# Half of retention's gates computed by block products, with retention's chunk in another order

## The chip, the cores and the metric

The kernel runs on one core of one Trainium2 chip. A core has TensorE (PE, matrix products into PSUM, which has eight banks), VectorE (DVE), ScalarE (ACT), GpSimd (POOL) and SyncE (SP, whose queue issues most DMAs). Each engine works through its own instructions in program order; semaphores let one wait for another. The metric is the time of one execution in microseconds (us) on the device.

## The reference

A decoder block on 1024 tokens of width 1024. After a modulated RMS norm, one wide projection `w_in` gives queries, keys, values and gates for four retention heads (key width 256, value width 512), queries, keys and values for twelve attention heads, and two merging gates. What the change touches, cut to its core:

```python
proj = h @ w_in
rq, rk, rv, rg = parts[0], parts[1], parts[2], parts[3]      # rg: 2048 gate columns, 512 a head
def step(state, inp):                                        # chunks of 128 tokens, 8 a head
    qi, ki, vi = inp
    s = einsum(qi, ki) * inner_decay
    o = einsum(s, vi) + einsum(qi, state) * q_decay
    state = state * chunk_decay + einsum(ki * k_decay, vi)
    return state, o
ro = (ro - mean(ro)) * rsqrt(var(ro) + GN_EPS)               # per head and token
ret_out = (silu(rg) * (ro * gn_g + gn_b)) @ w_ret_out
```

Then come dilated attention in three groups, the gated merge, an output projection, and an MLP with squared ReLU, each with its norm. The conditioning vector gives 48 column sets of modulation factors, `silu(c) @ w_ada`.

## The kernel before

**Arithmetic.** Each float32 operand is split into a rounded high half (ACT) and the remainder as low half (DVE); a product is three PE matmuls, low x high, high x low and high x high (`mm3`, L197). The rows L201, L203 and L205 of the profile are these three. A block of 128 input columns by 512 tokens takes three matmuls of 512 columns.

**Block products.** The class `Blocks` (L220 on) computes a pair of column sets (256 outputs) over 1024 inputs and 1024 tokens as a two by two block product with seven products in place of eight: sums of blocks of the weights (DVE), split halves, seven times four `mm3`, and sums of the results. A pair takes 7 x 4 x 3 = 84 matmuls; the plain way takes 2 x 48 = 96. `queries_keys` (L1072) runs 18 such pairs, in the order of `PAIRS` (L999): "r" rotated retention queries and keys, "a" attention queries, "g" merging gates (sigmoid). Results go to DRAM. `values` (L1182) follows: 14 products by blocks of retention's values, each of four parts `p`, whose results `v_post` (L1152) writes to DRAM; the low halves of the next weights come between the parts.

**Retention.** `chunk` (L672) is called for four heads h and eight chunks c; g = 8h + c. Everything is scheduled by hand: each engine executes in the order of the program's text. A chunk has, on PE: `kv` (keys by values, six matmuls), gate products `rg` (a set of 128 gate columns, 48 matmuls, over two chunks, 24 each), scores and key transposes of the next chunk (`s_kt`, L616), output `o` (six matmuls with the state, three with the scores), and transposes of the normalized result of the chunk before (`on_T`, L649). On DVE: the state update (two halves), the score steps, the keys' low half, the state's low half, mean and variance of `o`, the normalization itself (L728) at the chunk's end, and a modulation product (`mod_prep`, L449), one in each of 32 chunks. On ACT: high halves, copies of the transposed result, SiLU of a finished gate set (L732), and `u_final` (L660), which scales a set of the head before. On POOL: the low half of the next query and key tile `j` (L613) and a power. `ahead(2)` (from `Steps.run`, L72) splits the weights and does the modulation product of the next step at the place where it is called: in the middle of the chunk, ahead of `s_kt`. `fetch` (L583) loads queries, keys and values three chunks ahead.

**PSUM.** In retention four of the eight banks form two double tiles ("mm", `ps_mm`, L160), which the gate sets use in turn; the other four are single tiles ("s", `ps_s`, L163), taken in the order in which they come free by `kv` (two), `sT`, `kT`, `o` and `oT`. Before retention all eight banks are single tiles.

**The way in.** `values` ends with closing the memory pool of its tiles, opening retention's pool over the same memory (`open_ret`, L514), fetching chunks 1 and 2, scores of chunk 0 (`s_kt(0)`) and the new PSUM pool (`banks(False)`). A tile of the new pool waits until the old tiles under it are done with.

Of the kernel before, what the change touches and what calls it, by code (L numbers as in the profile page):

```python
# [40 lines left out]
CS_QD = 132  # L41
CS_QD2 = 136
# [92 lines left out]
def block_kernel(ctx, tc, io, stop=None, dbg=None):  # L135
# [342 lines left out]
    def proj_mm(ps, w, ks=range(NK)):  # L478
        outs = ps if isinstance(ps, list) else [ps[:, 0, :], ps[:, 1, :]]
        for k in ks:  # L480
            mm3(outs, wk(w, k), hx[k], k == 0, k == NK - 1)
# [32 lines left out]
    def open_ret():  # L514
        x_ctx.close()
        R["p"] = ret_ctx.enter_context(tc.tile_pool(name="ret", bufs=1, reuse_waits="tile"))
        R["state"] = R["p"].tile([P, 2, DV], F32, name="state")
        R["sh"] = R["p"].tile([P, 2, DV], F32R, name="stateh")
        R["sl"] = R["p"].tile([P, 2, DV], F32R, name="statel")

    def etile(name, dt=F32):
        return R["p"].tile([P, 1024], dt, tag="E", bufs=12, name=name)
# [82 lines left out]
    def jit_qk(i):  # L605
        src = hd["qk", i]
        if i > 1:
            t = R["p"].tile([P, 2, 4, C], F32R, tag="j", bufs=2, name=f"j{i}")
# [7 lines left out]
    def s_kt(i):  # L616
# [15 lines left out]
        sm = p.tile([P, C], F32, tag="sm", bufs=1, name=f"sm{h}{c}")  # L632
        smh = p.tile([P, C], F32R, tag="smh", bufs=2, name=f"smh{h}{c}")
        sml = p.tile([P, C], F32R, tag="sml", bufs=2, name=f"sml{h}{c}")
        nc.scalar.copy(sm, ps[:, :C])  # L635
        nc.vector.tensor_add(sm, sm, ps[:, C:2 * C])
        nc.vector.tensor_mul(sm, sm, decay[:, h * C:(h + 1) * C])
        nc.scalar.copy(smh, sm)
        nc.vector.tensor_sub(sml, sm, fv(smh))
        hd["s", g] = (smh, sml)  # L640
        if pk is not None:
            kd = ct[:, CS_KDEC + h:CS_KDEC + h + 1]
            kh = p.tile([P, 2, P], F32R, tag="kh", bufs=1, name=f"kh{h}{c}")
            kl = p.tile([P, 2, P], F32R, tag="kl", bufs=1, name=f"kl{h}{c}")
            nc.scalar.mul(kh, pk, kd)
            nc.vector.scalar_tensor_tensor(flat(kl), flat(pk), kd, fv(flat(kh)), op0=ALU.mult, op1=ALU.subtract)
            hd["k", g] = (kh, kl)
# [12 lines left out]
    def u_final(h, es=range(4)):  # L660
        for e in es:
            i = h * 4 + e
            t = hd["on", h][e]
            for hf in range(2):
                neg = 16 if hf == i % 2 else 0
                b = t[:, 512 * hf:512 * hf + 512]
                nc.scalar.activation(b, b, AF.Identity, scale=gnv[0][:, neg + i:neg + i + 1],
                                     bias=gnv[1][:, neg + i:neg + i + 1])
            nc.vector.tensor_mul(t, t, hd["srg", h, e])
            nc.sync.dma_start(y_d[:, 2 * (i % 2):2 * (i % 2) + 2, i // 2], t.rearrange("p (t x) -> p t x", t=2))  # L670

    def chunk(h, c, ahead, w=None):  # L672
# [4 lines left out]
        if c % 2 == 0:  # L677
            hd["rgw"] = w
            hd["rgp"] = ps_mm(f"rg{h}{c}")
        ks = range(4 * (c % 2), 4 * (c % 2) + 4)  # L680
        if g == 0:
            proj_mm(hd["rgp"], hd["rgw"], ks)
        vh, vl = hd["v", g][:, 0], hd["v", g][:, 1]
        st, sh, sl = R["state"], R["sh"], R["sl"]
        kvs = []
        if c < NC - 1:
            kh, kl = hd["k", g]
            for i in range(2):
                kv = ps_s(f"kv{h}{c}{i}")
                mm3([kv], (kh[:, i, :], kl[:, i, :]), [(vh, vl)], True, True)  # L690
                kvs.append(kv)
        if g > 0:
            proj_mm(hd["rgp"], hd["rgw"], ks[:2])
        for i, kv in enumerate(kvs):
            if c == 0:
                nc.vector.tensor_copy(st[:, i, :], kv)
            else:
                nc.vector.scalar_tensor_tensor(st[:, i, :], st[:, i, :], float(GAMMA[h] ** C), kv,
                                               op0=ALU.mult, op1=ALU.add)
        ahead(2)  # L700
# [8 lines left out]
        if c < NC - 1:  # L709
            for i in range(2):  # L710
                nc.scalar.copy(sh[:, i, :], st[:, i, :])
                nc.vector.tensor_sub(sl[:, i, :], st[:, i, :], fv(sh[:, i, :]))
        if g + 2 < NG:
            jit_qk(g + 2)
        if g > 0:
            on_T(*divmod(g - 1, NC))
        if g > 0:
            proj_mm(hd["rgp"], hd["rgw"], ks[2:])
# [5 lines left out]
        nc.vector.tensor_scalar(gr, ba[:, 1:2], ct[:, CS_QD2 + h:CS_QD2 + h + 1], GN_EPS, op0=ALU.mult, op1=ALU.add)  # L724
        nc.gpsimd.tensor_tensor(gr, gr, mhalf[:, 0:1], op=ALU.pow)
        nc.vector.tensor_mul(gr, gr, ct[:, CS_QD + h:CS_QD + h + 1])
        on = p.tile([P, DV], F32, tag="on", bufs=1, name=f"onm{h}{c}")
        nc.vector.tensor_scalar(on, po, ba[:, 0:1], gr, op0=ALU.subtract, op1=ALU.mult)  # L728
        hd["o", h, c] = on
        if c % 2 == 1:  # L730
            hd["srg", h, c // 2] = etile(f"srg{h}{c // 2}")
            nc.scalar.activation(hd["srg", h, c // 2], flat(hd["rgp"]), AF.Silu)  # L732
        if h > 0 and c < 4:
            u_final(h - 1, (c,))
# [264 lines left out]
    PAIRS = [{"r": r_pairs, "a": a_pairs, "g": g_pairs}[i].pop(0) for i in "rargrargrargrargaa"]  # L999
# [1570 lines left out]
```

## Time and profile before

| what | us |
|---|---|
| median of three runs (2231.76 to 2233.54) | 2232.41 |
| the profiled execution | 2231.9 |
| its span, first to last instruction | 2230.1 |
| PE busy | 2168.7 |
| DVE busy | 1470.1 |
| ACT busy | 912.4 |
| POOL busy | 155.1 |
| block products of queries, keys and gates | 149 to 492 |
| values | 492 to 647.4 |
| retention | 647.4 to 970.5 |

How to read it: the profiled execution lies 0.5 us below the median. A row of the order of time has start, duration, engine, line, operation, output and inputs; in brackets, how long the engine stood idle before and what released it. A row of a group has least, median and most duration in nanoseconds. A row of stages has the stretch, its length, busy time with instructions of PE, PE's weight loads, DVE, ACT and POOL, the granted PE clock as a share of full speed, the share of the DMA engines that was busy, and GB/s. PE's matmuls overlap, so the duration of one is longer than its share of time.

### The profile page before, as it was taken

The numbers are of one execution on the slowest core, as the hardware profiler recorded it, in microseconds if no ns is written. First come the engines' busy times: TensorE is split into PE (matmuls) and PEld (weight loads), VectorE is DVE, ScalarE is ACT, GpSimd is POOL, SyncE is SP. The second block draws the span as 40 slices with busy tenths as digits, with TensorE's granted clock in tenths as the row PEclk, the third lists the DMA queues.
The fourth block names the chain that finished last, engine by engine and source line by source line (L and its number), as shares of the span: only waits on it lengthen the run. The fifth ranks groups of instructions, "written<-read, shape, count | busy, mean of one in ns | idle before, by whom it ended". The sixth has DMA issues, their size and how long they took to land.

```text
span 2230.1 us, 27097 instructions
## 1 busy us (share of the span) xinstructions
PE 2168.7 (97%) x10082; PEld 1796.1 (81%) x10082; DVE 1470.1 (66%) x2303; ACT 912.4 (41%) x1671; POOL 155.1 (7%) x176
## 2 busy tenths in 40 slices
PE   7999999999989999999999999999999999999998
PEld 5888888878868888888788788888778888788887
DVE  6756777754448778865555654676866665787845
ACT  4532233223324444544634633524444445533412
POOL 0100111000012112200000000002000000000003
PEclk9999999999999999999999999999999999999999
DMA  9869999634675556559723265654234444745322
GB/s 383 220 208 299 294 296 277 189 131 174 224 255 170 181 178 203 185 175 238 224 73 96 92 219 187 237 180 159 69 135 147 155 156 165 261 141 170 123 85 76
DMA packets 157602, 414.15 MB, mean 186 GB/s; under 512 B 27222, under 2 KB 55133, under 8 KB 153054
## 3 DMA queue, kind: packets, MB, share of 16 engines
q1 hardware_dynamic: 149598, 364.19, 46.5%
q0 software_dynamic: 7872, 48.24, 9.5%
q8 instruction: 79, 1.29, 0.2%
q14 instruction: 53, 0.43, 0.1%
HBM read 321.51 MB, written 156.13 MB: 214 GB/s over the span
## 4 chain that ended last, share of the span: by engine, by line
PE 86%; DVE 6%; DMA 4%; ACT 3%; issue 1%; POOL 0%; SPq 0%; POOLq 0%; DVEq 0%; ACTq 0%
PE qap L203 5%; PE qap L201 5%; PE qap L205 5%; PE fp L201 4%; PE fp L203 4%; PE fp L205 4%; PE rg L201 3%; PE rg L203 3%; PE rg L205 3%; PE f2a L203 2%; PE f2a L205 2%; PE f2a L201 2%; PE ak L201 2%; PE ak L203 2%; PE ak L205 2%; PE va L203 1%
## 5 line engine op out<-in xcount | busy, mean ns | idle before, releaser
L201 PE MATMUL qap<-hh,qaw 128*128 128x512 f32 x216 | 84.1, 390 | 0.4 <-DVE qat L285 0.4
L205 PE MATMUL qap<-hh,qaw 128*128 128x512 f32 x216 | 84.0, 389 | 0.0
L203 PE MATMUL qap<-hl,qaw 128*128 128x512 f32 x216 | 84.0, 389 | 0.0
L613 POOL TENSOR_TENSOR j<-qk,j 128x512 fp32r<-128x512 f32 x32 | 43.3, 1353 | 462.2 <-ACT j L612 462.2
L2029 ACT ACTIVATE a<-a 128x512 f32<-128x512 f32 x48 | 30.3, 632 | 79.5 <-DVE a L2028 79.5
L1926 POOL TENSOR_TENSOR accnf<-accnf,sqnf 128x256 f32<-128x256 f32 (+1 forms) x18 | 16.6, 921 | 620.2 <-ACT sqnf L1925 620.2
L1383 ACT ACTIVATE P<-P,ng 128x128 f32<-128x128 f32 (+1 forms) x96 | 41.9, 438 | 39.0 <-DVE ng L1380 39.0
L258 DVE TENSOR_TENSOR fw<-w1r,fw 128x512 fp32r<-128x512 f32 x48 | 32.9, 687 | 36.2 <-ACT fw L248 36.2
L2215 ACT CAST w2h<-w2s 128x512 fp32r<-128x512 f32 x36 | 22.3, 621 | 77.6 <-DVE w2s L2253 73.6
L635 ACT COPY sm<-sT 128x128 f32<-128x128 f32 x32 | 8.5, 265 | 111.0 <-PE sT L626 103.8
L201 PE MATMUL fp<-h2h,fw 128*128 128x512 f32 x128 | 50.0, 390 | 0.0
L203 PE MATMUL fp<-h2l,fw 128*128 128x512 f32 x128 | 49.8, 389 | 0.0
L205 PE MATMUL fp<-h2h,fw 128*128 128x512 f32 x128 | 49.8, 389 | 0.0
L201 PE MATMUL roa<-rh,rwl 128*128 128x512 f32 x128 | 49.8, 389 | 0.0
L203 PE MATMUL roa<-rl,rwh 128*128 128x512 f32 x128 | 49.8, 389 | 0.0
L205 PE MATMUL roa<-rh,rwh 128*128 128x512 f32 x128 | 49.8, 389 | 0.0
L1764 DVE TENSOR_TENSOR rwl<-rwl,rwh 128x1024 fp32r<-128x1024 f32 x25 | 30.2, 1220 | 29.1 <-ACT rwh L1794 29.1
L1926 POOL TENSOR_TENSOR accn<-accn,sqn 128x512 f32<-128x512 f32 x12 | 15.5, 1293 | 478.2 <-ACT sqn L1925 478.2
L201 PEld LDWEIGHTS qap<-hh,qaw 128*128 128x128 f32 x216 | 40.5, 188 | 9.2 <-DVE qat L285 0.8
L203 PEld LDWEIGHTS qap<-hl,qaw 128*128 128x128 f32 x216 | 40.5, 188 | 8.4
L205 PEld LDWEIGHTS qap<-hh,qaw 128*128 128x128 f32 x216 | 40.5, 188 | 8.4
L258 DVE TENSOR_TENSOR qaw<-wa,qaw 128x512 fp32r<-128x512 f32 x54 | 37.0, 686 | 10.0 <-ACT qaw L248 10.0
(3063 smaller groups left out, 7188.1 us busy)
## 6 DMA issues: line engine op xcount, KB each, us to landing
v<-vd SPq DMA_DIRECT2D x32, 512.0 KB, 4.8
raw<-in_w_ada_dram SPq DMA_DIRECT2D x32, 512.0 KB, 5.1
w1r<-in_w_ff_dram SPq DMA_DIRECT2D x32, 512.0 KB, 4.8
vd<-vo SPq DMA_DIRECT2D x24, 512.0 KB, 4.4
yt<-y POOLq DMA_DIRECT2D x6, 2048.0 KB, 16.5
xsd<-as SPq DMA_DIRECT2D x24, 512.0 KB, 2.7
w2r<-in_w_ff2s_dram SPq DMA_DIRECT2D x24, 512.0 KB, 7.3
em<-in_w_ada_dram SPq DMA_DIRECT2D x16, 512.0 KB, 10.2
```

What stands on the lines that cost most here:

```text
L201: nc.tensor.matmul(o, wl, xh, start=first, stop=False, skip_group_check=skip)
L203: nc.tensor.matmul(o, wh, xl, start=False, stop=False, skip_group_check=skip)
L205: nc.tensor.matmul(o, wh, xh, start=False, stop=last, skip_group_check=skip)
L258: nc.vector.tensor_sub(t[:, 512:], src, fv(t[:, :512]))
L613: nc.gpsimd.tensor_sub(t[:, 1], src, fv(t[:, 0]))
L635: nc.scalar.copy(sm, ps[:, :C])
L1383: nc.scalar.activation(v, v, AF.Exp, bias=ng[:, blk:blk + 1], accum_out=st[:, g, blk, 2 + a:3 + a])
L1764: nc.vector.tensor_sub(lo, fv(lo), fv(hi))
L1926: (nc.vector if f == 7 else nc.gpsimd).tensor_add(G["acc", key], G["acc", key], sq)
L2029: nc.scalar.activation(o, o, AF.Relu)
L2215: nc.scalar.copy(hi, src)
```

## The change

- Of each head's four gate sets the last two (256 columns) become a pair "s" in `PAIRS`: 22 pairs in place of 18, results through SiLU to DRAM (`srg_d`). Retention computes only the first two, each over four chunks (12 matmuls a chunk; in chunks 0 to 3 of head 0: 24, 12, 6 and 6), and loads the other two in chunks 6 and 7 of their head.
- Within a chunk: normalization is put off to the next chunk (`normed`, with the mean folded into a bias `nb`, and done by ACT); the transposes are of the result two chunks back; state update and state halves are done 1024 wide, both products `kv` in one double tile; the keys' halves come ahead of the scores'; `u_final` is cut into `u_scaled` (ACT, early in the chunk) and `u_gated` (DVE). `ahead(2)` is called ahead of `s_kt` as before, but in chunks with c % 4 = 3 at the chunk's end, behind SiLU.
- A constant `CS_EPS` replaces two scale factors of the normalization.
- Thirteen of the 32 modulation products go to `values` (`v_mod`), with their loads; the other 19 stay: in head 0 in chunks 1 to 7, in the others in chunks 0, 1, 2 and 7.
- The way in: the small tiles of `s_kt` are allocated first in retention's pool; `s_kt(0)` comes in chunk 0 behind the first half of its gate products; these take the odd input tiles first, since the even ones are being restored from DRAM; the last values product takes its parts in the order 3, 0, 1, 2.
- Tile counts: "E" 11 for 12, "j" 3 for 2.

```diff
     def proj_mm(ps, w, ks=range(NK), order=range(NK)):
         outs = ps if isinstance(ps, list) else [ps[:, 0, :], ps[:, 1, :]]
+        for i in ks:
+            mm3(outs, wk(w, order[i]), hx[order[i]], i == 0, i == NK - 1)
...
+        for n in R_SMALL:
+            R[n] = r_small(n, "00")
...
+    R_SMALL = {"sm": ([P, C], F32, 1), "kh": ([P, 2, P], F32R, 1), "kl": ([P, 2, P], F32R, 1), "smh": ([P, C], F32R, 2),
+               "sml": ([P, C], F32R, 2)}
...
+    def normed(g):
+        h, c = divmod(g, NC)
+        po, ba, gr = hd["o", h, c]
+        nb = R["p"].tile([P, 1], F32, tag="nb", bufs=2, name=f"nb{h}{c}")
+        nc.vector.scalar_tensor_tensor(nb, ba[:, 0:1], -1.0, gr, op0=ALU.mult, op1=ALU.mult)
+        on = R["p"].tile([P, DV], F32, tag="on", bufs=2, name=f"onm{h}{c}")
+        nc.scalar.activation(on, po, AF.Identity, scale=gr, bias=nb)
+        hd["o", h, c] = on
     def chunk(h, c, ahead, w=None):
...
+        if c % 4 == 0:
             hd["rgw"] = w
             hd["rgp"] = ps_mm(f"rg{h}{c}")
+        if c in (6, 7):
+            hd["srg", h, c - 4] = etile(f"srg{h}{c - 4}")
+            nc.sync.dma_start(hd["srg", h, c - 4], srg_d[h][c - 6])
+        ks = ((0, 1, 2, 3), (4, 5), (6,), (7,))[c] if g < 4 else range(2 * (c % 4), 2 * (c % 4) + 2)
+        late = int(c % 4 > 0)
+        gated = h > 0 and 1 < c < 6
         if g == 0:
+            proj_mm(hd["rgp"], hd["rgw"], ks[:2], (1, 3, 5, 7, 0, 2, 4, 6))
+            s_kt(0)
+            proj_mm(hd["rgp"], hd["rgw"], ks[2:], (1, 3, 5, 7, 0, 2, 4, 6))
+        elif g + 2 < NG:
+            jit_qk(g + 2)
+        if gated:
+            u_scaled(h - 1, c - 2)
...
         if c < NC - 1:
             kh, kl = hd["k", g]
+            kv = ps_mm(f"kv{h}{c}")
             for i in range(2):
+                mm3([kv[:, i]], (kh[:, i, :], kl[:, i, :]), [(vh, vl)], True, True)
         if g > 0:
+            proj_mm(hd["rgp"], hd["rgw"], ks[:late], (1, 3, 5, 7, 0, 2, 4, 6))
+        if c == 0:
+            nc.vector.tensor_copy(flat(st), flat(kv))
+        elif c < NC - 1:
+            nc.vector.scalar_tensor_tensor(flat(st), flat(st), float(GAMMA[h] ** C), flat(kv),
+                                           op0=ALU.mult, op1=ALU.add)
+        if g > 0:
+            normed(g - 1)
+        if gated:
+            u_gated(h - 1, c - 2)
+        if c % 4 < 3:
+            ahead(2)
         if g + 1 < NG:
             s_kt(g + 1)
...
         mm3([po], hd["s", g], [(vh, vl)], c == 0, True)
         if c < NC - 1:
+            nc.scalar.copy(flat(sh), flat(st))
+        if g > 1:
+            on_T(*divmod(g - 2, NC))
         if g > 0:
+            proj_mm(hd["rgp"], hd["rgw"], ks[late:], (1, 3, 5, 7, 0, 2, 4, 6))
...
+        hd["o", h, c] = po, ba, gr
+        if c < NC - 1:
+            nc.vector.tensor_sub(flat(sl), flat(st), fv(flat(sh)))
+        if c % 4 == 3:
+            hd["srg", h, c // 4] = etile(f"srg{h}{c // 4}")
+            nc.scalar.activation(hd["srg", h, c // 4], flat(hd["rgp"]), AF.Silu)
+            ahead(2)
+        if g == 0:
+            jit_qk(g + 2)
...
+    PAIRS = [{"r": r_pairs, "a": a_pairs, "g": g_pairs, "s": s_pairs}[i].pop(0) for i in "rsrarsrarsrarsraggagga"]
...
+    def v_mod(i):
+        t, j = cs[:, i % 2], VMODS[i]
+        nc.vector.scalar_tensor_tensor(t, t, 1.0, cb, op0=ALU.mult, op1=ALU.mult, accum_out=mods[:, j:j + 1])
+        nc.vector.tensor_add(mods[:, j:j + 1], mods[:, j:j + 1], vec[:, VC_BADA + j:VC_BADA + j + 1])
...
+            if i < last:
+                nc.sync.dma_start(cs[:, i % 2], io["w_ada"][VMODS[i]])
...
+                if p == (1 if i == last else 3) and i > 0:
+                    v_mod(i - 1)
```

More of the change, by code (lines that the diff above doesn't have):

```diff
@@ L40 @@
 CS_KDEC = 128
-CS_QD = 132
-CS_QD2 = 136
+CS_EPS = 132
 CS_ONE = 140
@@ L723, in chunk @@
         nc.vector.bn_aggr(ba, bn)
-        nc.vector.tensor_scalar(gr, ba[:, 1:2], ct[:, CS_QD2 + h:CS_QD2 + h + 1], GN_EPS, op0=ALU.mult, op1=ALU.add)
+        nc.vector.tensor_add(gr, ba[:, 1:2], ct[:, CS_EPS + h:CS_EPS + h + 1])
         nc.gpsimd.tensor_tensor(gr, gr, mhalf[:, 0:1], op=ALU.pow)
[L726 to L734, printed above, removed]
+        hd["o", h, c] = po, ba, gr
[7 more added lines that the diff above has]
+            jit_qk(g + 2)
     def wsplit(ap):
@@ L1216, in values @@
             fetch(g)
-        s_kt(0)
         banks(False)
```

113 lines of the change are left out of this document (51 added, 62 removed).

## The prediction

> **What bounds the kernel now.** I read the page first, then busy time by stage, then the order of time of one retention chunk and of the way into retention. In the page, the engine that does the work nearly all the time:
>
> ```profile
> span 2230.1 us, 27097 instructions
> PE 2168.7 (97%) x10082; PEld 1796.1 (81%) x10082; DVE 1470.1 (66%) x2303; ACT 912.4 (41%) x1671; POOL 155.1 (7%) x176
> ```
>
> TensorE (PE) is the bound. The profiled execution took 2231.9 us, 0.5 below the median of the runs shown (2232.41). By stage: block products of queries, keys and gates; values; the way into retention (chunks 0 and 1 of head 0); the rest of retention.
>
> ```profile
> 149.00:492.00 343.00, 342.63 (x1512) 283.40 (x1511) 244.56 (x383) 99.96 (x171) 33.63 (x48) 1.00 0.80 249
> 492.00:647.40 155.40, 153.33 (x679) 126.65 (x677) 73.28 (x87) 60.06 (x84) 7.11 (x10) 1.00 0.63 223
> 647.40:682.50 35.10, 22.45 (x95) 17.96 (x95) 17.11 (x37) 8.79 (x22) 3.18 (x3) 0.81 0.61 206
> 682.50:970.50 288.00, 288.00 (x1405) 239.65 (x1404) 229.46 (x479) 133.48 (x336) 54.16 (x59) 1.00 0.53 176
> ```
>
> PE is the first busy column, VectorE (DVE) the third, ScalarE (ACT) the fourth. 343.00 us for 1512 products of 512 columns is **0.2268 us** a product, the price used below; a matmul's own duration, 0.39, overlaps its neighbours. Retention fills PE wholly, except on the way in. One chunk of head 0, PE alone (first matmul of each part):
>
> ```profile
> 702.38 0.39 PE L201 MATMUL kv<-v,kl 128*128 128x512 f32 x1
> ...
> 703.75 0.61 PE L201 MATMUL rg<-hh,raw_4971l 128*128 128x512 f32 x2
> ...
> 706.47 0.28 PE L624 MATMUL sT<-j 128*128 128x256 f32 x1
> ...
> 707.02 0.48 PE L201 MATMUL o<-stateh,j 128*128 128x512 f32 x1
> ...
> 709.20 0.60 PE L656 MATMUL oT<-ct,onm 128*128 128x128 f32 x4
> 709.55 0.71 PE L201 MATMUL rg<-hh,raw_4971l 128*128 128x512 f32 x2
> ...
> 712.39 0.39 PE L201 MATMUL kv<-v,kl 128*128 128x512 f32 x1
> ```
>
> So: kv 1.37, scores and key transposes 0.55, output 2.18 (with its six state products; 0.73 without, as in c = 0), result transposes 0.35, and 24 gate products. And the way in:
>
> ```profile
> 655.97 0.27 ACT L635 COPY sm<-sT 128x128 f32<-128x128 f32 x1 [7.20 <-DMA vd<-vr]
> ...
> 658.15 1.22 PE L201 MATMUL rg<-hh,raw_4651l 128*128 128x512 f32 x2 [10.13 <-DVE kl L646]
> ```
> ```profile
> 656.00:658.00 2.00, 0.00 (x0) 0.00 (x0) 1.26 (x4) 0.90 (x3) 0.00 (x0) 0.50 1.02 345
> ...
> 660.00:661.00 1.00, 1.00 (x4) 0.78 (x3) 0.00 (x0) 0.00 (x0) 0.00 (x0) 0.50 0.26 99
> ...
> 662.00:663.00 1.00, 1.00 (x6) 0.79 (x5) 0.00 (x0) 0.00 (x0) 0.00 (x0) 1.00 0.05 16
> ```
>
> `sm` waits for the store of a values result whose memory it takes over; the first gate product waits for `kl`, since the new PSUM pool lays it over the bank of `kT`. Then PE starts at a granted clock of 0.50.
>
> **The change, part by part.** Durations that the parts use (nanoseconds: least/median/most): the two halves of a weight split, a modulation product with its two small steps, a 1024 wide difference from PSUM, a one-column operation, an activation with scale and bias from memory.
>
> ```profile
> L191 ACT CAST raw_4651h<-raw x1: 1042/1042/1042, 634.4 to 634.4; 128x1024 fp32r<-128x1024 f32 x1
> ...
> L192 DVE TENSOR_TENSOR raw_4651l<-raw,raw_4651h x1: 1227/1227/1227, 635.4 to 635.4; 128x1024 fp32r<-128x1024 f32 x1
> ...
> L452 DVE SCALAR_TENSOR_TENSOR raw<-raw,cb x32: 1212/1218/1222, 636.6 to 958.0; 128x1024 f32<-128x1024 f32 x32
> L452 DVE DVE_READ_ACCUMULATOR raw<-raw,cb x32: 79/81/87, 637.7 to 959.1; 128x1 f32 x32
> ...
> L454 DVE TENSOR_TENSOR mods<-mods,vec x32: 158/159/163, 637.8 to 959.2; 128x1 f32<-128x1 f32 x32
> ...
> L1330 DVE TENSOR_TENSOR kl<-ak,kh x12: 1211/1224/1225, 987.6 to 1213.2; 128x1024 fp32r<-128x1024 f32 x12
> ...
> L724 DVE TENSOR_SCALAR gr<-ba,ct x32: 212/214/217, 672.7 to 970.8; 128x1 f32<-128x1 f32 x32
> ...
> L667 ACT ACTIVATE on<-on,gnt x32: 807/840/853, 749.3 to 984.5; 128x512 f32<-128x512 f32 x32
> ```
>
> *Products.* Eight of 16 gate column sets leave retention: 8 x 48 = 384 products. Four pairs by blocks add 4 x 7 x 4 x 3 = 336. Net 48 x 0.2268 = **-10.9**. The pairs' other work (splits, sums, SiLU, a 512 KB store per column set) is that of the four gate pairs now in this stage, whose DVE is busy 245 of 343 us and ACT 100: cost 0; if that cover failed, PE would wait at bank changes. Retention's reload of them, two per head on SP's queue, comes four chunks ahead of use: 0.
>
> *Thirteen modulation products* go from retention to values, where DVE is busy 73 of 155.4 us: 13 x 1.46 more makes 92. Cost 0; their loads queue on SP behind the next weights, so the result stores come a little later. Without DVE's slack the next low halves would be late.
>
> *Way in.* 72 products, three score parts and one of result transposes in chunks 0 and 1 need 72 x 0.2268 + 3 x 0.55 + 0.35 = 18.3 of 35.2 us: 16.9 lost. The scores now come behind the first 12 gate products, in the new pool, and `sm` lies elsewhere. What is late next is `kl` of chunk 1, behind its score chain (about 1), and the loads of `v` and `qk`, behind the same stores. I take 3 left: **-14**. Bounds: -16 (loads in time) and -5 (`sm`'s new place is again under a late store; the key product then waits instead of the gate product, hidden for 6 us).
>
> *Chunk order.* A chunk needs on PE 27 x 0.2268 + 0.55 + 0.14 + 0.35 = 7.2, with the loose ends of the trace 7.3. DVE had 229.46 us in 288, 8.0 a chunk, and 10.67 in a heavy one of head 1, from one normalization to the next:
>
> ```profile
> 751.01 0.81 DVE L728 TENSOR_SCALAR onm<-o,ba,gr 128x512 f32<-128x512 f32 x1
> ...
> 761.68 0.81 DVE L728 TENSOR_SCALAR onm<-o,ba,gr 128x512 f32<-128x512 f32 x1
> ```
>
> It loses the normalization (to ACT), 13 of 32 modulations (0.6 a chunk) and half of the gate splits (0.3): about 6.4, so in ordinary chunks PE still bounds. There the normalization of g-1 ends at 3.8 (kv 1.55 with its tail, state 1.22 as `kl<-ak,kh`, `nb` 0.2 as `gr`, normalization 0.8), and the transposes that take over its bank come at 2 x 1.37 + 0.55 + 2.18 = 5.45: cost 0. ACT has 133.48 us in 288, 4.7 a chunk, and takes the 0.8: 0. Of the E tiles, one fewer now, a head holds eight; each new one finds one that the gated product of the same chunk has freed: 0.
>
> *Chunks with c % 4 = 0, the largest term.* In the chunk ahead, SiLU waits for the last gate product, and only behind it come, in program order, the split's high half (ACT), its low half (DVE), a modulation (DVE; at c = 0, and at c = 4 of head 0), and then the new chunk's state update (DVE), `nb` (DVE), the normalization (ACT). All four single banks are taken: scores, key transposes and output hold three, the raw result of g-1 the fourth, until it is normalized. So the transposes of g-2 wait for this chain, and the gate products queue behind them.
>
> ```profile
> 702.58 1.03 ACT L732 ACTIVATE srg<-rg 128x1024 f32<-128x1024 f32 x1 [1.69 <-PE rg L205]
> ```
>
> From the new chunk's start (as 702.38 to 702.58 above): SiLU 0.2 to 1.23, high half to 2.3, low half to 3.5, modulation to 4.9, state (1024 wide from PSUM) to 6.1, `nb` to 6.3, normalization (an estimate between `gr`'s 0.21 and L667's 0.84, near the latter, which also has scale and bias from memory) 0.8 to 7.1. PE is there at 1.37 + 0.55 + 0.73 = 2.65 for c = 0, 4.1 for c = 4. Waits: c = 0, heads 1 to 3: 7.1 - 2.65 = 4.5 each; c = 4 of heads 1 to 3, without modulation: 5.7 - 4.1 = 1.6 each. In head 0 chunk 3 has only six gate products, ahead of the scores, and ends on PE with the transposes; ahead of SiLU ACT then has their copies and a table load, since the gate pairs' sigmoid has put out SiLU's table:
>
> ```profile
> 978.89 0.77 ACT on L658 x4
> ...
> 983.76 2.72 DMA y<-on
> ```
> ```profile
> 681.84 1.28 ACT L732 ACT_TABLE_LOAD   x1
> ```
>
> All is 0.77 + 1.28 later there: 9.1 - 4.1 = 5.0. Sum 13.5 + 4.8 + 5.0 = **+23**. The next chunk then runs without a wait, as DVE and ACT have caught up.
>
> *What comes on top.* In these chains GpSimd (POOL) takes the low half of `j` of g+2 (1.3 us, two SBUF inputs), released by ACT's high half of `j` behind the split's, at 2.3 + 0.6 = 2.9, in the midst of DVE's low half. How the two go together:
>
> ```profile
> L612 ACT CAST j<-qk x32: 607/620/627, 629.8 to 953.2; 128x512 fp32r<-128x512 f32 x32
> ```
> ```profile
> 630.52 1.47 POOL L613 TENSOR_TENSOR j<-qk,j 128x512 fp32r<-128x512 f32 x1 [205.68 <-ACT j L612]
> 632.29 1.29 POOL L613 TENSOR_TENSOR j<-qk,j 128x512 fp32r<-128x512 f32 x1 [0.30 <-ACT j L612]
> ```
> ```profile
> 632.34 2.31 DVE L1137 TENSOR_TENSOR vwl<-vwl,vwh 128x1024 fp32r<-128x1024 f32 x1
> ```
>
> DVE's operation, begun 0.05 after POOL's, took 2.31 and not 1.22: it stood still for POOL's. Here POOL would wait for the low half and then hold up the modulation by up to 1.3, four times: 0 to 5, taken 4 (the row is the same operation). The Trainium skill, "SBUF — State Buffer", section "Who interferes with whom", says that a VectorE instruction with two SBUF inputs and a GpSimd one that reads SBUF share a port pair, which whoever issues first holds to its end; the trace agrees (2.31). By it the state update, with one input in PSUM, would not wait, and the three waits of 1.6 would stay.
>
> A wait of some 5 us also costs clock. The nearest row, a wait of 5.29, with the clock in the column before the last two:
>
> ```profile
> 1642.01 0.80 PE L201 MATMUL fp<-xt,fw 128*128 128x512 f32 x1 [5.29 <-DVE ft2h2t L285]
> ```
> ```profile
> 1640.00:1642.00 2.00, 0.00 (x0) 0.00 (x0) 1.93 (x5) 0.62 (x1) 0.00 (x0) 0.74 0.16 60
> ...
> 1646.00:1648.00 2.00, 2.00 (x7) 1.57 (x6) 2.00 (x4) 0.69 (x2) 0.00 (x0) 0.55 0.03 9
> ```
>
> The clock fell about 4.2 us into the wait and stayed at half for 5.6 us after it: 2.8 us lost. Four waits here are 4.5 to 6.3 long: 0 to 11, taken 4 (half of them fall low, a little more briefly). The Trainium skill, "TensorE: Matmul & The Clock Gate", section "HAM oscillation — how this bites in real kernels", wants no idle gap over about 3.4 us; by it all four would pay, as an estimate some 7 in all, at its half rate for one such stretch each.
>
> *End of retention.* Two transposed results instead of one come behind the first four key products, and the attention's tiles wait for the last store of the gated results (`y<-on`, on the chain above); ACT, ahead of it on that chain, has four more copies (0.77): **+1** (0 to 2).
>
> Sum: 2231.9 - 10.9 - 14 + 23 + 4 + 4 + 1 = 2239.0; with the 0.5 to the median **2239.5**, 0.3% slower. Its own range: with the on-top terms at nothing and the best way in, 2232.4 - 10.9 - 16 + 23 = 2228.5; with all of them and the bad way in, 2232.4 - 10.9 - 5 + 23 + 5 + 11 + 2 = 2257.5; both at once are rare: 2230 to 2251.
>
> **The rivals.**
>
> *Faster: the waits at c % 4 = 0 are short.* The chain is read from program order and from a bank count of four. If the transposes found a free bank (the scores' bank, say), or the split were done a chunk earlier, the wait would go and 2232.4 - 10.9 - 14 + 1 = 2208 would be left. For it: DVE has 0.9 us of slack in a mean chunk. Against: the bank of the scores is read by ACT behind the normalization. It decides early: my sum without on-top terms is 2230.5, so at 20 us for the seven places instead of 23 (2.9 each instead of 3.3) and no lost clock it is already faster by over 0.2%.
>
> *The way in is not mended.* `sm` or the state lands under a result still being stored (four of 26 slots hold such): +9, 2248.
>
> *DVE bounds ordinary chunks too.* With a modulation or a gated product, c = 0 to 6 of head 0 and c = 2 to 5 of the others exceed the mean by up to 1.2 us, and POOL's hold comes on top once a chunk: 7.6 or more against 7.3. At 0.5 for 24 chunks +12: 2251. For it: the heavy chunk above, which now fills DVE. Against: a late chunk is followed by a lighter one.
>
> **How the numbers follow.** Likeliest 0.51, faster rival 0.29, way in 0.12, DVE 0.08. What a measurement of this kernel can tell from no change is about 0.2%, 4.5 us: 2227.9 to 2236.9. The likeliest case gives 0.02 faster, 0.14 same, 0.35 slower; the faster rival 0.28 faster and 0.01 same; the others slower but for 0.01. So faster 0.30, same 0.16, slower 0.54. The range, 2209 to 2252, leaves out a tenth at each end.
>
> **What would show it.** 336 products more in the block stage at 0.2268. No PE wait of 10 us at the way in, and the clock at 1.00 there. Seven PE waits before `oT` (L656's successor), released by the normalization on ACT: near 4.5 to 5.8 us three times, 5.0 to 6.3 once, 1.6 three times, with dips of the clock; ordinary chunks at 7.3. Wrong it would be if those waits ended at something else or were under 2 us, if ordinary chunks took over 7.6, or if values grew beyond 156 us.

## The result, and the profile after

The changed kernel took **2254.69 us** (median of four runs, 2249.36 to 2257.84), the kernel before 2232.12 beside it: ratio 1.0097, 95% interval 1.0077 to 1.0118, 1% slower. The prediction had the sign and most of the terms, but said 2239.5, with a range that ended at 2252. The profiled execution took 2255.98.

The page of the changed kernel:

```profile
span 2254.0 us, 27033 instructions
PE 2169.7 (96%) x10034; PEld 1794.9 (80%) x10034; DVE 1473.4 (65%) x2271; ACT 948.3 (42%) x1707; POOL 181.1 (8%) x176
```

PE has 48 matmuls fewer and is no less busy, a first sign that matmuls ran slowly somewhere. By stage (columns as in the prediction: length, busy time of PE, its weight loads, DVE, ACT and POOL, granted clock, share of the DMA engines, GB/s): block products; values; the way in (chunks 0 and 1); the rest of retention; the attention's keys up to the first scores; the rest of attention.

```profile
149.10:568.60 419.50, 419.26 (x1850) 346.89 (x1850) 286.58 (x447) 128.58 (x219) 33.62 (x48) 1.00 0.71 224
568.60:723.30 154.70, 152.63 (x674) 126.11 (x673) 87.91 (x123) 59.27 (x84) 8.00 (x10) 1.00 0.73 262
723.30:741.00 17.70, 14.38 (x72) 11.56 (x71) 12.21 (x21) 6.12 (x13) 4.00 (x3) 1.00 0.99 356
741.00:988.90 247.90, 219.89 (x1053) 181.18 (x1051) 182.66 (x367) 144.51 (x331) 79.03 (x59) 0.94 0.55 182
988.90:1006.30 17.40, 17.40 (x74) 14.32 (x75) 7.31 (x8) 10.39 (x20) 0.00 (x0) 0.90 0.45 156
1006.30:1358.00 351.70, 337.67 (x1817) 286.54 (x1815) 189.69 (x290) 162.40 (x363) 6.89 (x8) 1.00 0.53 163
```

The same cuts of the kernel before, ahead of attention and in it:

```profile
148.90:492.30 343.40, 343.03 (x1513) 283.71 (x1512) 244.66 (x383) 99.96 (x171) 33.63 (x48) 1.00 0.80 249
...
972.60:988.00 15.40, 15.40 (x71) 12.77 (x70) 7.67 (x8) 11.07 (x18) 0.00 (x0) 1.00 0.42 150
988.00:1333.90 345.90, 335.48 (x1815) 285.22 (x1814) 188.02 (x288) 161.33 (x363) 6.89 (x8) 1.00 0.54 163
```

Blocks +76.1, values -0.4, retention with its way in 265.6 against 325.2, that is -59.6, first keys +2.0, attention +5.8: together the 23.9 by which the spans differ. Retention lost 384 products, 87.1 us, and with the way in it should have lost 101; 41 us came back inside it. PE's waits there:

```profile
PE oT L664 <- ACT onm L693: 24.7, 7, 6.0
PE ak L200 <- DVE raw_7516l L191: 3.3, 1, 3.3
PE kv L200 <- DVE kl L651: 2.2, 1, 2.2
PE sT L635 <- POOL j L624: 1.1, 1, 1.1
```

24.7 us in seven waits before the transposes, released by the normalization. One of them, c = 0 of head 2, in order of time. The new chunk begins at 856.36 (its first `kv`).

```profile
852.79 0.78 ACT L693 ACTIVATE onm<-o,nb,gr 128x512 f32<-128x512 f32 x1 [2.25 <-DVE nb L691]
...
856.56 1.03 ACT L764 ACTIVATE srg<-rg 128x1024 f32<-128x1024 f32 x1 [0.62 <-PE rg L204]
...
857.49 1.04 ACT L190 CAST raw_6182h<-raw 128x1024 fp32r<-128x1024 f32 x1
...
858.55 1.23 DVE L191 TENSOR_TENSOR raw_6182l<-raw,raw_6182h 128x1024 fp32r<-128x1024 f32 x1 [2.51 <-ACT raw_6182h L190]
...
859.17 1.73 POOL L624 TENSOR_TENSOR j<-qk,j 128x512 fp32r<-128x512 f32 x1 [2.44 <-ACT j L623]
859.70 2.28 DVE L451 SCALAR_TENSOR_TENSOR raw<-raw,cb 128x1024 f32<-128x1024 f32 x1
...
862.10 1.22 DVE L728 COPY state<-kv 128x1024 f32<-128x1024 f32 x1
...
863.23 0.15 DVE L691 SCALAR_TENSOR_TENSOR nb<-ba,gr 128x1 f32<-128x1 f32 x1
...
863.42 0.78 ACT L693 ACTIVATE onm<-o,nb,gr 128x512 f32<-128x512 f32 x1 [4.38 <-DVE nb L691]
...
864.25 1.11 PE L664 MATMUL oT<-ct,onm 128*128 128x128 f32 x4 [5.02 <-ACT onm L693]
```

It is the chain of the prediction, link by link: SiLU, high half, low half, modulation (2.28 and not 1.22, since POOL's `j` runs into it), state update, `nb`, normalization. It ends 7.8 us after the chunk's start; 7.1 was read, with up to 1.3 for POOL on top. The transposes themselves read the result of two chunks back, which the first row wrote some 10 us earlier: what they wait for is not their data but the bank that the normalization at 863.42 reads. What comes behind the wait was underrated: the clock. Here it is, first in stretches of 3.41 us around this wait, then at the instant of its fall at four places (PEclk stands before the last two numbers):

```profile
860.03:863.45 3.42, 0.00 (x0) 0.00 (x0) 3.39 (x6) 0.03 (x1) 0.87 (x1) 1.00 0.48 163
863.45:866.86 3.41, 2.61 (x8) 2.24 (x9) 3.27 (x11) 2.86 (x8) 0.00 (x0) 0.50 0.92 322
866.86:870.27 3.41, 3.41 (x9) 2.64 (x8) 1.19 (x2) 0.94 (x3) 2.66 (x2) 0.50 1.06 379
870.27:873.69 3.42, 3.42 (x20) 2.88 (x18) 1.81 (x3) 0.48 (x1) 0.00 (x0) 1.00 0.17 65
```
```profile
764.40:764.50 0.10, 0.00 (x0) 0.00 (x0) 0.10 (x1) 0.07 (x1) 0.00 (x0) 0.80 1.30 246
798.50:798.60 0.10, 0.00 (x0) 0.00 (x0) 0.10 (x3) 0.00 (x0) 0.00 (x0) 0.97 0.47 82
863.40:863.50 0.10, 0.00 (x0) 0.00 (x0) 0.10 (x1) 0.08 (x1) 0.00 (x0) 0.73 0.00 0
928.30:928.40 0.10, 0.00 (x0) 0.00 (x0) 0.10 (x1) 0.10 (x1) 0.00 (x0) 0.51 0.39 41
```

A slice of 0.1 us at 0.80 is full for 0.06 and half for the rest: the falls lie at 764.46, 798.59, 863.45 and 928.30. They are 34.13, 64.85 and 64.85 apart: 10, 19 and 19 times 3.413. The falls at 989.7 and 1160.4 (below) lie 18 and 68 such steps behind the last of them. The clock is judged on a fixed grid of 3.413 us, not from the wait's end, and each wait of 5 or 6 us cost two steps at half speed, 6.83 us, of which the first 0.8 to 0.9 were still idle: **3.0 us lost, at all four places**. The Trainium skill, "TensorE: Matmul & The Clock Gate", section "What's actually happening", states a free-running window of 4096 cycles at 1.2 GHz, 3413 ns; the trace agrees (34.13 us for ten).

Between the boundaries nothing is lost: in the rest of retention PE was idle 247.90 - 219.89 = 28.0 us, the 24.7 at the boundaries and the 3.3 at the end. The key transposes of chunks 1, 2 and 3 of head 2 begin 7.28 apart:

```profile
873.47 0.40 PE L642 MATMUL kT<-ct,qk 128*128 128x128 f32 x2
...
880.75 0.40 PE L642 MATMUL kT<-ct,qk 128*128 128x128 f32 x2
...
888.03 0.40 PE L642 MATMUL kT<-ct,qk 128*128 128x128 f32 x2
```

At the end of retention the attention's first key weights are late, since their split stands behind the last SiLU, as at the other boundaries; behind that wait the clock is at half for one step, from 989.7, which costs 1.7.

```profile
985.59 1.02 ACT L764 ACTIVATE srg<-rg 128x1024 f32<-128x1024 f32 x1 [0.63 <-PE rg L204]
...
986.51 1.04 ACT L190 CAST raw_7516h<-raw 128x1024 fp32r<-128x1024 f32 x1
...
987.58 1.23 DVE L191 TENSOR_TENSOR raw_7516l<-raw,raw_7516h 128x1024 fp32r<-128x1024 f32 x1 [2.71 <-ACT raw_7516h L190]
...
988.86 0.72 PE L200 MATMUL ak<-hh,raw_7516l 128*128 128x512 f32 x2 [3.31 <-DVE raw_7516l L191]
```

So of the 41 us: 24.7 waits, 4 x 3.0 clock, 3.3 at the first keys; that makes 40.0. (The 1.7 of the last step falls behind the first key product, in the +2.0 of the first keys.)

### The profile page after: what moved, and what is told of

Read it like the earlier page. It is cut to its first block, busy times and chain, and to the rows that moved or that the text cites. A ratio compares the mean times of both kernels' runs of the same rounds, so it can differ in the third digit from the quotient of the medians.

```text
span 2254.0 us, 27033 instructions
## 1 busy us (share of the span) xinstructions
PE 2169.7 (96%) x10034; PEld 1794.9 (80%) x10034; DVE 1473.4 (65%) x2271; ACT 948.3 (42%) x1707; POOL 181.1 (8%) x176
## 4 chain that ended last, share of the span: by engine, by line
PE 82%; DVE 8%; ACT 4%; DMA 3%; issue 1%; POOL 0%; SPq 0%; POOLq 0%; DVEq 0%; ACTq 0%
PE qap L200 6%; PE qap L204 6%; PE qap L202 6%; PE fp L200 4%; PE fp L202 4%; PE fp L204 4%; PE f2a L202 2%; PE f2a L204 2%; PE f2a L200 2%; PE ak L200 2%; PE ak L202 2%; PE ak L204 2%; PE rg L200 1%; PE rg L202 1%; PE rg L204 1%
## 5 line engine op out<-in xcount | busy, mean ns | idle before, releaser
L200 PE MATMUL qap<-hh,qaw 128*128 128x512 f32 x264 | 102.8, 390 | 0.2 <-DVE qat L284 0.2
L204 PE MATMUL qap<-hh,qaw 128*128 128x512 f32 x264 | 102.7, 389 | 0.0
L202 PE MATMUL qap<-hl,qaw 128*128 128x512 f32 x264 | 102.7, 389 | 0.0
L693 ACT ACTIVATE onm<-o,nb,gr 128x512 f32<-128x512 f32 x32 | 24.9, 778 | 80.7 <-DVE nb L691 80.7
L200 PEld LDWEIGHTS qap<-hh,qaw 128*128 128x128 f32 x264 | 49.6, 188 | 10.8 <-DVE qat L284 0.7
L204 PEld LDWEIGHTS qap<-hh,qaw 128*128 128x128 f32 x264 | 49.6, 188 | 10.4
L202 PEld LDWEIGHTS qap<-hl,qaw 128*128 128x128 f32 x264 | 49.6, 188 | 10.3
L257 DVE TENSOR_TENSOR qaw<-wa,qaw 128x512 fp32r<-128x512 f32 x66 | 45.0, 686 | 18.2 <-ACT qaw L247 18.2
L758 POOL TENSOR_TENSOR gr<-gr,ct 128x1 f32<-128x1 f32 x32 | 41.4, 1293 | 167.7 <-DVE gr L757 167.7
L247 ACT CAST qaw<-wa 128x512 fp32r<-128x512 f32 x66 | 39.7, 617 | 27.9 <-PE qap L204 21.8
```

The costliest lines, as they stand in the source:

```text
L200: nc.tensor.matmul(o, wl, xh, start=first, stop=False, skip_group_check=skip)
L202: nc.tensor.matmul(o, wh, xl, start=False, stop=False, skip_group_check=skip)
L204: nc.tensor.matmul(o, wh, xh, start=False, stop=last, skip_group_check=skip)
L247: nc.scalar.copy(t[:, :512], src)
L257: nc.vector.tensor_sub(t[:, 512:], src, fv(t[:, :512]))
L693: nc.scalar.activation(on, po, AF.Identity, scale=gr, bias=nb)
```

## The experiments

All edits are to the changed kernel. "Retention" is from the first gate product to the first key product of attention (in the kernel before, whose first gate product waited for 10.1 us, from the end of values), "attention" from there to the first product of the merge. Both are from the one profiled execution, which took between 3.4 us less (the last run) and 8.3 us more than the run's median ("the same, gate products first" with 2227.6).

| run | median us | ratio to before, 95% | retention | attention |
|---|---|---|---|---|
| before | 2232.4 | | 325.4 | 361.3 |
| the change | 2254.7 | 1.0097, 1.0077 to 1.0118 | 265.4 | 369.1 |
| gate products first | 2238.0 | 1.0025, 1.0013 to 1.0036 | 248.2 | 371.5 |
| split and modulation in mid-chunk | 2228.9 | 0.9985, 0.9973 to 0.9998 | 242.5 | 362.1 |
| waits filled | 2242.6 | 1.0043, 1.0026 to 1.0060 | 254.4 | 365.3 |
| `j` late | 2246.3 | 1.0060, 1.0045 to 1.0075 | 258.5 | 365.8 |
| modulations moved | 2242.6 | 1.0037, 1.0024 to 1.0050 | 252.8 | 371.4 |
| small tiles late | 2256.2 | one run | 265.4 | 365.3 |
| both in mid-chunk, behind the scores | 2236.1 | 1.0009, 0.9997 to 1.0022 | 248.6 | 365.3 |
| the same, gate products first | 2227.6 | 0.9978, 0.9965 to 0.9990 | 241.6 | 370.9 |
| only the split in mid-chunk | 2230.1 | 0.9987, 0.9979 to 0.9996 | 241.9 | 364.2 |
| the same, gate products first, `j` late | 2222.5 | 0.9956, 0.9944 to 0.9968 | 232.3 | 367.5 |
| the same, `j` early | 2217.4 | 0.9938, 0.9923 to 0.9954 | 229.9 | 364.1 |

**Is it the clock?** The waits filled with products that nobody needs:

```diff
+        for _ in range(20 if c == 0 and g > 0 else 24 if g == 4 else 0):
+            nc.tensor.matmul(hd["rgp"][:, 0, :], hh[0][:, :P], hh[0][:, :512], start=True, stop=True, ...)
         if g > 1:
             on_T(*divmod(g - 2, NC))
```

> Edit to the changed kernel: in the four chunks with the long waits, products that nobody needs (20, and 24 in chunk 4 of head 0) stand ahead of the transposes, written to the gate bank that the gate products then begin anew; the result is the same. They take 4.5 and 5.4 us of waits of 5.0 and 6.0. Theory A: the transposes begin no earlier, PE doesn't stand still for over 1 us, the granted clock stays at 1.00: only the clock's 4 x 3.1 = 12.4 us goes, 2254.7 falls to about 2242. Rival B (the slow stretch behind the waits is not from idleness): no change, 2255. If the extra products delay the chain: slower than 2257.

2242.6, as theory A had it. The transposes still come behind the normalization (a wait of 0.5), but PE has worked until then, and the 15 us around that place are at full clock (first row: stretches; second: order of time):

```profile
789.00:804.00 15.00, 14.49 (x70) 11.81 (x69) 11.24 (x22) 6.99 (x17) 4.99 (x4) 1.00 0.59 196
```
```profile
798.31 0.66 PE L664 MATMUL oT<-ct,onm 128*128 128x128 f32 x4 [0.51 <-ACT onm L693]
```

84 products more, 12 us less (11.0 of it within retention): the loss behind the waits is the clock's.

**Is it that bank?** The transposes behind the gate products:

```diff
-        if g > 1:
+        if g > 1 and c % 4:
             on_T(*divmod(g - 2, NC))
         if g > 0:
             proj_mm(hd["rgp"], hd["rgw"], ks[late:], ...)
+        if g > 1 and c % 4 == 0:
+            on_T(*divmod(g - 2, NC))
```

> Only edit to the changed kernel: in chunks with c % 4 = 0 the transposes of g-2 come behind the chunk's 12 gate products instead of ahead of them. Theory A (the wait is for the bank that the normalization frees, and each wait of 5 to 6 us costs another 3.1 us of TensorE clock): 12 x 0.2268 = 2.7 us of work moves into the wait, so 5.0 becomes 2.3 three times, 6.0 becomes 3.3, 1.2 vanishes three times: 14.5 us less idle. Waits of 2 to 3 us leave the clock at 1.00: 4 x 3.1 = 12.4 more. 2254.7 falls to about 2228. Rival B (the time lost behind the waits isn't the clock's, but contention or late operands): the idle time goes, the rest stays: 2240. Rival C (the gate products are themselves late, for the low half of their weights): the wait only changes its place: over 2248.

2238.0: the gain is 17 and not 27. The gate products don't need that bank and now fill the wait. Most of the wait is covered, but it broke up into three (0.61 for the weights' low half, 1.44 for the normalization, 0.79 for `kl` of the next chunk), and three of the four places still lost one step of the clock. Where rival B's 2240 is near, it is so for another reason: filled waits show that the clock was the price.

**What the chain is made of.** First the split and the modulation, put back into mid-chunk:

```diff
-        if c % 4 < 3:
-            ahead(2)
+        ahead(2)
 ...
             nc.scalar.activation(hd["srg", h, c // 4], flat(hd["rgp"]), AF.Silu)
-            ahead(2)
```

> Only edit to the changed kernel: the next weights' split (and modulation) of chunks 3 and 7 stands in mid-chunk, where the other chunks have theirs, instead of behind SiLU. Theory A: at a boundary the chain is now state update (to 2.8 us), its small step (2.95) and the normalization (3.8), PE is there at 2.65 or 4.1: waits of 1.2 us three times, the other four gone, so 24.7 - 3.6 = 21.1; no clock drop there, 12.4; the first key weights are ready at the end of retention, 3.3 + 2.2. Together 39: 2254.7 falls to about 2216. Rival D (DVE is too full in chunk 3 for another 1.2 us): a new wait of about 1 us at each of four chunks, and 2220 or more. Rival B (lost time is not the clock's): 2230.

2228.9, not 2216. The boundary waits fell to 5.4 in all and the 3.3 at the first keys went, as theory A had it. Rival D was right too, at another instruction: split and modulation now stand ahead of the keys' low half on DVE, and the next chunk's key products wait for it.

```profile
757.20 0.80 PE L200 MATMUL kv<-v,kl 128*128 128x512 f32 x1 [3.06 <-DVE kl L651]
...
789.38 0.50 PE L200 MATMUL kv<-v,kl 128*128 128x512 f32 x1 [1.55 <-DVE kl L651]
```

Then the modulation alone, due at c = 5 in place of c = 0:

```diff
-  ([mod_load(later_mods.pop(0))] if c in (1, 2, 7) or (c > 0 if h == 0 else c == 0) else [])
+  ([mod_load(later_mods.pop(0))] if c in (1, 2, 5, 7) or (c > 0 and h == 0) else [])
```

> Only edit to the changed kernel: the modulation product that heads 1 to 3 have at c = 0 is due at c = 5 instead, so it stands in mid-chunk of c = 4 and no longer in the chain at the boundary. Theory A: 2.4 us (2.28 with POOL's hold, and its small steps) leave the chain, and POOL's operation then lies beside the state update, which reads PSUM and isn't held: waits of 5.0 become 2.6 three times, 7.2 less. If a wait of 2.6 us leaves the clock at 1.00, 3 x 3.1 more goes: 2238; if the clock falls all the same, as it did behind a wait of 3.06 in the run with the split in mid-chunk, only about half of that: 2243. Rival F (DVE has no room for it in chunk 4, whose key low half then comes late, 1.5 us as in the run with the split in mid-chunk): 4.5 us come back.

The three waits are 2.62, and the time is 2242.6: the clock fell behind two of the three. Equal waits, unequal price: the step that held most of the wait was idle for 2.12 and 2.56 us where the clock fell, and for 1.90 where it did not, so the price goes by how the grid cuts the wait.

Then POOL's part, `j` behind the normalization:

```diff
-        elif g + 2 < NG:
+        elif g + 2 < NG and c % 4:
             jit_qk(g + 2)
 ...
             normed(g - 1)
+        if g > 0 and c % 4 == 0 and g + 2 < NG:
+            jit_qk(g + 2)
```

> Only edit to the changed kernel: in chunks with c % 4 = 0 the halves of j for g+2 (high on ACT, low on POOL) stand behind the normalization instead of at the chunk's head, so POOL's subtraction no longer lies in the chain. Theory A (POOL's operation holds the modulation up for 1.05 us, 2.28 instead of 1.22, and the state update, that reads PSUM, not at all): waits of 5.0 become 4.0 three times, 6.0 becomes 4.9, the three of 1.2 stay: 4.2 less, and with waits of 4 us the clock hardly drops, up to 9 more: 2241 to 2251. Rival E (the 2.28 is DVE's own, from something else): no change, 2255.

2246.3. The seven waits are 20.5 in place of 24.7, the 4.2 foreseen, and the modulation takes 1.22 again:

```profile
857.69 1.22 DVE L451 SCALAR_TENSOR_TENSOR raw<-raw,cb 128x1024 f32<-128x1024 f32 x1
```

**What mended the way in?** The small tiles taken at first use again:

```diff
-        for n in R_SMALL:
-            R[n] = r_small(n, "00")
```

> Only edit to the changed kernel: the small tiles of the scores and keys (sm, smh, sml, kh, kl) are not set out when the retention pool opens but taken at first use, as in the kernel before; the order of the way in stays that of the change. Theory G (the place of the small tiles mended the way in): sm again waits some 8 us for a store of a values result; 24 gate products cover 6 of it, and the key products wait about 2 to 4 us in chunk 0. Rival H (the order alone mended it, the gate products ahead of the scores): no wait over 1 us before the key products of chunk 0, the 2.2 and 1.1 us of chunk 1 as they are.

Rival H: PE's waits at the way in are the same 2.2 and 1.1. The order mended it without the tiles' place; my reason, that `sm` lies elsewhere, was not the cause. Which part of the order did it (the gate products ahead of the scores, the odd input tiles first, the parts of the last values product in the order 3, 0, 1, 2), no run separates.

**Can the order be had without its price?** Split and modulation behind the scores' small operations in all chunks, then the same with the gate products first (the edit above):

```diff
-        if c % 4 < 3:
-            ahead(2)
         if g + 1 < NG:
             s_kt(g + 1)
+        ahead(2)
 ...
-            ahead(2)
```

> Edit to the changed kernel: split and modulation stand in mid-chunk in all chunks, behind the scores' and keys' small operations instead of ahead of them. Against the run with the split in mid-chunk (2228.9), whose key products waited for the low half of kl (1.55 us three times, 3.06 once with a clock drop of about 3, 2.2 at chunk 1): kl comes ahead of the split, so 4.65 + 3.06 + 3 and about 1.4 of the 2.2 go, 12 in all: 2217. The waits of 1.3 and 0.5 for the normalization stay. Rival I (the statistics, now behind split and modulation, make pow and the normalization late instead): the waits for the normalization grow by over 1 us, and 2225 or more.

> As the run before it in this list (split and modulation behind the scores' small operations), and in chunks with c % 4 = 0 the transposes also stand behind the 12 gate products. Theory A: the waits of 1.3 and 0.5 for the normalization, three each, are covered too: 5.4 less than that run, 2212, and no long wait is left in retention; both kernels are beaten. Rival J (the transposes' bank comes free later, so that the next scores wait): no gain over that run, 2217.

2236.1 and 2227.6. Rival I was right: the statistics of `o` come behind split and modulation, and with them the normalization; at c = 0 the wait was 3.7 three times, each with a step of half clock. The gate products first took 8.5 off that (7.0 in retention), more than the 5.4 expected, since the three steps of half clock went with the waits of 3.7. But 13 us of smaller waits were left in retention, among them 2.6 for the state's low half in chunk 4 of head 0, which now also comes behind the split.

Only the split in mid-chunk, the modulation left behind SiLU (`ahead`'s second argument takes weights alone); then with the gate products first and `j` late; then with `j` early:

```diff
-        if c % 4 < 3:
-            ahead(2)
+        ahead(2, c % 4 == 3)
```

> Edit to the changed kernel: in chunks 3 and 7 only the split of the next weights stands in mid-chunk (ahead of the scores), the modulation stays behind SiLU. Theory A: against the run with both in mid-chunk (2228.9) the low half of kl is late by about 0.3 us instead of 1.55 (three times), and 1.6 instead of 3.06 with its clock drop of 3.4 (chunk 4 of head 0); the modulation ends within 0.9 us of the new chunk, ahead of the state update: waits for the normalization 1.3 and 0.5, three each, as they were. Sum 3.8 + 1.5 + 3.4 = 8.7 less: 2220. No window of PE is idle for more than half, so the clock stays at 1.00 in retention. Rival I (the order of DVE's work only moves the wait: state update behind the modulation, normalization later by 1.5): waits of 2.8 three times, clock drops in some of them: 2228 or more.

> The run before it in this list, and in chunks with c % 4 = 0 the transposes behind the 12 gate products and the halves of j behind the normalization. Theory A: the rest of the boundary waits is covered, 5.4 less than that run: 2215, 0.8% less than the kernel before. Rival J (key products of the next chunk wait for kl instead, 0.8 us at each of seven places, as where the gate products alone were put first): 2220.

> The fastest run so far (weights' split in mid-chunk, transposes behind the gate products, 2222.5) with the halves of j back at the chunk's head. There POOL's subtraction, behind the normalization, lay over the scores' product sm on DVE (1.05 us instead of 0.29), and the next key products waited 0.9 us for kl. Theory K (POOL's place makes that wait): with j early, POOL runs beside the state update, which reads PSUM; kl comes 0.8 us earlier at seven places, 5 us less: 2217. Rival L (POOL then holds up the small step ahead of the normalization instead, by up to 1.1 us, or the modulation at c = 0): no gain or a loss, 2222 to 2227.

2230.1 (rival I again: 1.89 at c = 0, 2.02 in chunk 4 of head 0, and two steps of half clock), 2222.5 and **2217.4**. In the second, every boundary wait is gone but the key products wait for `kl` (rival J), because POOL's subtraction now lies over a small DVE operation with two operands in SBUF; first the run with `j` late, then `j` early, both at c = 0 of head 1:

```profile
792.06 1.29 POOL L624 TENSOR_TENSOR j<-qk,j 128x512 fp32r<-128x512 f32 x1 [2.46 <-ACT j L623]
...
792.45 1.05 DVE L646 TENSOR_TENSOR sm<-sm,decay 128x128 f32<-128x128 f32 x1
...
793.95 0.50 PE L200 MATMUL kv<-v,kl 128*128 128x512 f32 x1 [0.93 <-DVE kl L651]
```
```profile
787.77 1.22 DVE L728 COPY state<-kv 128x1024 f32<-128x1024 f32 x1
788.02 1.29 POOL L624 TENSOR_TENSOR j<-qk,j 128x512 fp32r<-128x512 f32 x1
788.90 0.43 DVE L691 SCALAR_TENSOR_TENSOR nb<-ba,gr 128x1 f32<-128x1 f32 x1
...
790.91 0.29 DVE L646 TENSOR_TENSOR sm<-sm,decay 128x128 f32<-128x128 f32 x1
...
791.65 0.50 PE L200 MATMUL kv<-v,kl 128*128 128x512 f32 x1 [0.17 <-DVE kl L651]
```

`sm` took 1.05 beside POOL and 0.29 without; beside the state update, which reads PSUM, POOL's operation costs only 0.28 of `nb`. With that the waits for `kl` fell from 7.8 to 5.4 in all, and retention by 2.4, where theory K had 5; the rest of the 5.2 between the medians lies outside retention, which the edit doesn't touch, so that 2217 was met is in part luck. Retention of that last run, at full clock throughout:

```profile
723.20:953.10 229.90, 223.42 (x1121) 184.68 (x1121) 195.52 (x386) 146.29 (x342) 81.66 (x61) 1.00 0.67 223
```

Against the change it moves two things, the split and the transposes, and it beats both kernels, the one before by 0.6% (0.5 to 0.8).

## Why the prediction was right and wrong

| step | predicted | measured |
|---|---|---|
| products, net | -10.9 | +76.1 in the blocks, 48 matmuls fewer: right |
| modulations in values | 0 | -0.4: right |
| way in | -14 | 3.3 left of 16.8 lost, clock 1.00: -13.5, right |
| ordinary chunks | 7.3 | 7.28: right |
| seven waits, with POOL's hold | +23 and +4 | 24.7, of it 4.2 POOL's: right, 2.3 less |
| lost clock behind them | +4 (0 to 11) | 12.0: **wrong** |
| end of retention and attention | +1 (0 to 2) | 3.3 + 2.0 + 5.8 = 11.1: **wrong** |

*Waits.* They were where and what the prediction had said: 5.02 three times (4.5 to 5.8 foreseen), 5.96 (5.0 to 6.3), 1.23 three times (1.6). The four places where the low half of `j` meets the modulation also came out, 4.2 for 4.

*Lost clock*, the mis-sized term. "Half of them fall low, a little more briefly": all four fell, and by more than the 2.8 of the row used. The mechanism was right. The price of one was taken from a single earlier wait, and that half of the four would escape rested on no row; what a wait costs is one or two whole steps of a grid. A wait of over 3.55 us puts more than 1.77 us of idleness into some step wherever it lies (below), so none of the four could escape. The upper end of its bounds, 11, was short as well.

*End of retention.* I priced the transposes and the stores there and overlooked that `ahead(2)` of the last chunk splits the first weights of attention: the step "SiLU, high half, low half" was priced at seven boundaries, and the eighth, the way out, was left out. It cost 3.3 and one step of clock (the keys' 2.0, mostly that). All runs with the split in mid-chunk are without the 3.3 and its step.

*Attention*, +5.8 behind the keys, is only partly explained. The kernel before waits 0.8 for the gate's sigmoid `g00s`, the change 2.6; for the first merge product it waits 1.4 and the kernel before not at all; near 1160 the clock fell for one step, 1.7. That makes 4.9. The wait of 1.4 stands in ten of the eleven edits too. No edit touches this stage, yet it took 362.1 to 371.5 in the runs; only one of them, with split and modulation in mid-chunk, was as short as before, and being late at the keys does not separate the short from the long. In two of the long ones (modulations moved, and both behind the scores with gate products first) ACT stood idle for 5.5 and 5.0 us until the gate's weights were loaded, ahead of their split; in the change itself it did not. There is one trace of each kernel, and executions of one kernel differ by up to 12 us (2213.95 to 2226.40 for the last run), so how much of the 5.8 belongs to the change and how much to that one execution can't be told. What sets it stays open, and with it 1 to 10 us in each run.

*Rivals.* "The waits are short" had the fact wrong: they were 24.7. Moving two lines shortens them (242.5 of retention instead of 265.4), but no edit came to the 2208 of that rival; the fastest took 2217.4. "The way in is not mended" and "DVE bounds ordinary chunks" fell, by 2.2 and 1.1 at the way in and by 7.28.

With the clock at 12, and 5.3 at the way out, the prediction's own sum would have been 2239.5 + 8 + 4.3 = 2251.8. Most of the 2.9 left is attention's 5.8, less the 2.3 by which the seven waits were shorter than the sum had them.

Two slips in the working changed nothing: 2 x 1.37 + 0.55 + 2.18 is 5.47, not 5.45, and by its row the way in took 35.1, not 35.2, so 16.8 were lost.

## What to carry to other kernels

Price a wait of PE with its clock: here one over 3.5 us cost 1.7 to 3.0 us more every time, and one of 1.8 to 3.5 did so or not, by where it lay on the grid. Whatever is called behind an operation that waits for the last product of a set stands on the path of every such boundary, the way out of the loop included; list all of its call sites. Moving such preparation into the middle of a chunk only helps as far as the engine that does it has room there: ahead of the scores it made the keys' low half late, behind them the statistics, and the best of the places tried was the split alone ahead of the scores with the modulation left behind. Where a wait can't be removed, let products that don't depend on it go first.

## What the runs showed of the hardware

**About half a step of idleness is enough.** In retention and the first keys of the change and of the eleven edits, a grid step at full clock in which PE stood idle for 1.77 us or more was followed by half clock, 32 times, with one exception (1.90); with 1.75 or less it never was. The nearest to the border, the first from the run with gate products first, followed by half clock, the second from the one with all behind the scores and gate products first, not followed by it:

```profile
765.40:768.81 3.41, 1.62 (x8) 1.25 (x9) 3.31 (x11) 2.69 (x7) 0.00 (x0) 1.00 0.86 300
768.81:772.23 3.42, 3.42 (x10) 2.69 (x9) 3.28 (x6) 1.36 (x6) 2.66 (x2) 0.50 1.05 379
```
```profile
761.70:765.10 3.40, 1.65 (x7) 1.39 (x8) 3.21 (x6) 1.39 (x2) 2.66 (x2) 1.00 0.96 326
```

PE was busy 1.62 of 3.41 in the first and 1.65 in the second: about half decides, though the busy time here is modelled. In the first it was the end of one wait and another of 0.79 that added up. The Trainium skill, "TensorE: Matmul & The Clock Gate", section "HAM oscillation — how this bites in real kernels", gives the rule that no idle gap may exceed about 3.4 us; here sums half as long cost clock, and the measurement decides. In attention, with its small matmuls, single steps with 0.65 to 0.9 of idleness were also followed by half clock; why, no run here tells. Outside retention the border is less sharp, too: steps with 1.79 and 1.81 (in attention, with only the split in mid-chunk, gate products first and `j` late; at the end of the blocks, with split and modulation in mid-chunk) were not followed by half clock, one with 1.76 was (behind attention, with both behind the scores and gate products first).

**Port.** POOL's subtraction held up not only a 1024 wide DVE operation (2.28 for 1.22) but also one of 128 columns (1.05 for 0.29), and even `nb`, one column (0.43 for 0.15); beside one with an operand in PSUM (`state`, 1.22) neither was longer. The Trainium skill, "SBUF — State Buffer", section "Who interferes with whom", says so of two operands in SBUF, and the traces agree. In the other direction POOL's one-column power took 1.39 beside `statel` and 0.54 alone.
